# Two-layer encoder trunk on one core: a first phase with seven accumulators, six raw buffers and a fixed order

## The chip, the cores and the metric

The kernel runs on one core of a Trainium2 chip. The metric is the device time of one execution in microseconds (us). A core has five engines with instruction queues of their own: PE (matmul), DVE (elementwise, PSUM reads), ACT (activation functions, copies), POOL (elementwise on SBUF) and SP, which here only issues DMAs. An engine works through its queue strictly in the order in which the program was built, and waits at an instruction until its semaphores are up. Everything queued behind it waits too.

## The reference, cut to what matters

`x` is (1, 512, 1024). Layer 0 is built of a pooling mixer and a spatial-gating MLP, layer 1 of gated linear attention and stick-breaking attention. The change concerns the start of layer 0:

```python
def ada_modulate(x, c, norm_g, ada_w, ada_b):
    ada = jax.nn.silu(c) @ ada_w + ada_b
    shift, scale, gate = jnp.split(ada, 3, axis=-1)
    h = rmsnorm(x, norm_g) * (1.0 + scale[:, None, :]) + shift[:, None, :]
    return h, gate[:, None, :]

def even_layer(x, c, ...):
    h, gate_res = ada_modulate(x, c, norm_g, ada_w, ada_b)
    a, u, v, gate = _split(h @ in_w, EVEN_SIZES)
    ya = pool_mixer(a, pool_w, pool_scale)
    yb = spatial_gating(u, v, sgu_norm_g, sgu_w, sgu_b)     # u * (w . rmsnorm(v) + b)
    y = jnp.concatenate([ya, yb], axis=-1) * jax.nn.silu(gate)
    return x + gate_res * (y @ out_w)
```

So `h` (512 x 1024) is the left factor of one wide projection, and `ada` (a 1024-vector product per output column) must be there before `h` is. `u`, `v` and `gate` are column groups of that projection. `spatial_gating` normalises all of `v` (1024 columns) before it mixes tokens.

## The kernel before, in words

**Numbers.** The products are made in float32 accuracy out of reduced-precision matmuls: each operand is split into a high part (rounded, by ACT) and a low part (the difference, by DVE), and `mm3` issues three matmuls of 512 columns, high x high, high x low, low x high (lines L198, L199, L200). `split_w` (L184 on ACT, L185 on DVE) splits a weight tile into `whi` and `wlo`; `modulate` splits an activation tile into `hhi` (L305 or L307) and `hlo` (L308).

**First phase.** The contraction of 1024 is cut into eight k-tiles of 128. For each k-tile, `prepare(k)` does this: two `ada_block`s (each loads a 512 KB `raw` tile with the DMA of L167, and DVE reduces it against `sc`, the broadcast silu(c), with the custom operation of L174; L178 makes the scale `gcol`), one load of `wfirst` (768 columns: 512 of `v`, 256 of the gate) and its split, four transposes of the normalised x into an `aux` bank (L297), the modulation `h` (L301 or L303), `hhi` and `hlo`. Then 18 matmuls follow: four token blocks of `v` and two column blocks of the gate, each three matmuls, into six accumulators in the six `mm` banks of PSUM. `aux` has the two remaining banks. The `raw` tiles share four buffers, so a load is issued when the tile four loads earlier has been used up.

**Before the first phase** x comes in four token blocks (L149); ACT squares and sums each (L357), POOL turns the sum into 1/rms in two small operations (L282, L283), and DVE multiplies blocks 0 to 2 by it (L288), ACT block 3 (L362).

**After it** follow the other 512 columns of `v` (a unit of 96 matmuls in four accumulators), the 256 columns `u` of head group 0 (48 matmuls), then `gating` (eight float32 matmuls, L453, which read all four normalised blocks of `v`), `zs` on DVE and POOL (L456, L460) and the product with `u` (L464). Three more head groups and the pooling mixer go the same way, with further `ada_block`s put between the units as fillers, then the output projection and layer 1.

**What sets the order.** The program is written as straight code, and a scheduler orders the instructions of each engine when it is built, by its own estimate of times; it also decides which buffer a tile gets. On the chip nothing is reordered. Where the text says `manual_schedule`, the named engines keep the order in which the code is written.

Of the kernel before, what the change touches and what calls it, by code (L numbers as in the profile page):

```python
# [17 lines left out]
P = 128  # L18
# [21 lines left out]
def pack_inputs(i):  # L40
# [20 lines left out]
    g0 = 3072  # L61
    first = np.concatenate([w0[:, 2048:2560], w0[:, g0 + 1024:g0 + 1280]], axis=1).reshape(KT, P, 768)
# [35 lines left out]
def trunk(ctx: ExitStack, tc: tile.TileContext, d, out):  # L98
# [53 lines left out]
    for n in range(2):  # L152
        c = slice(n * 512, (n + 1) * 512)
        ps = bank("aux")
        T.matmul(ps, ones[0:1], c_row[0:1, c], start=True, stop=True)
        V.tensor_copy(out=sc[:, c], in_=ps)

# [132 lines left out]

    def modulate(l, k, tbs, xn):

        w = P * len(tbs)
        r = slice(tbs[0] * P, tbs[0] * P + w)
        ps = bank("aux")
        for i, t in enumerate(tbs):
            T.transpose(ps[:, i * P:(i + 1) * P], xn[t][:, k * P:(k + 1) * P], ident)  # L297
        h = slot("silu")
        g, b = gcol[:, 8 * l + k:8 * l + k + 1], ada[:, 24 * l + k:24 * l + k + 1]
        if l == 0 and k == 0:  # L300
            V.tensor_scalar(out=h, in0=ps, scalar1=g, scalar2=b, op0=ALU.mult, op1=ALU.add)  # L301
        else:
            A.activation(out=h[:, :w], in_=ps[:, :w], func=AF.Identity, scale=g, bias=b)  # L303
        if l or k:
            A.activation(out=h_hi[k][:, r], in_=h[:, :w], func=AF.Copy)  # L305
        else:
            V.tensor_copy(out=h_hi[k][:, r], in_=h[:, :w])  # L307
        V.tensor_tensor(out=h_lo[k][:, r], in0=h[:, :w], in1=h_hi[k].bitcast(F32)[:, r], op=ALU.subtract)  # L308

# [43 lines left out]

    xn = []
    for t in range(TB):
        n = big("n")
        A.activation(out=n, in_=x[t], func=AF.Square, accum_out=ss[:, t:t + 1])  # L357
        r = rms_scale(ss[:, t:t + 1], D)
        if t < TB - 1:
            normalise(t, r, n)  # L360
        else:
            A.mul(out=n, in_=x[t], mul=r)  # L362
        xn.append(n)

# [6 lines left out]
    v_ps = [bank() for _ in range(TB)]  # L371
    g_ps = [bank() for _ in range(2)]
    w_first = {}

    def prepare(k):
        ada_block(0, 8 + k)
        ada_block(0, k)
        w_first[k] = split_w(raw(d["wfirst"][k], 768), 768)
        modulate(0, k, range(TB), xn)
    prepare(0)  # L380
    for k in range(KT):
        if k + 1 < KT:
            prepare(k + 1)
        hi, lo = w_first.pop(k)
        for t in range(TB):
            r = slice(t * P, (t + 1) * P)
            mm3(v_ps[t], h_hi[k][:, r], h_lo[k][:, r], hi[:, :512], lo[:, :512], k == 0, k == KT - 1)
        for j in range(2):
            c = slice(512 + j * P, 512 + (j + 1) * P)
            mm3(g_ps[j], hi[:, c], lo[:, c], h_hi[k], h_lo[k], k == 0, k == KT - 1)  # L390

# [48 lines left out]
    for g in range(4):  # L440
# [380 lines left out]
```

## Time and profile before

| what | value |
|---|---|
| median of 3 runs | 865.55 us (864.79 to 869.39) |
| the profiled execution's own time | 867.59 us |
| its span, first to last instruction | 865.9 us |
| PE busy | 831.5 us, 96% |
| DVE, ACT, POOL busy | 503.0, 388.8, 82.1 us |
| DMA | 108.31 MB, 125 GB/s over the span |

PE is the engine to follow. Its busy time counts from issue to a modelled end, so that a matmul of 0.39 us that is followed by the next after 0.23 us counts as gapless work. The useful views are therefore the list of PE's waits, and the start times of its instructions, which show the pace. In a timeline a row gives the start, the duration, the engine, the line, the operation, what is written and read, and in brackets the idle time before it with what ended it. In the table by stretches a row gives the length, the busy time and the number of records of each engine, the granted clock of PE, and the share and rate of the DMA engines.

### The profile page before, as it was taken

How to read it: one execution, taken by the hardware profiler on the slowest of the kernel's cores; microseconds unless marked ns; L12 is line 12 of the kernel's file. 1: busy time of each engine (PE TensorE's matmuls, PEld its weight loads, DVE VectorE, ACT ScalarE, POOL GpSimd, SP SyncE). 2: the span in 40 equal slices, each digit the busy share in tenths (PEclk: the TensorE clock that was granted, in tenths of full speed). 3: DMA queues.
4: the chain of work that ended last, by engine and by line, in shares of the span. 5: the costliest groups of instructions: out<-in, count | busy, mean ns of one | idle time of the engine just before them, and what ended most of it. 6: DMA issues, size and time to landing. Idle time of an engine off the chain costs nothing.

```text
span 865.9 us, 10023 instructions
## 1 busy us (share of the span) xinstructions
PE 831.5 (96%) x3720; PEld 661.2 (76%) x3720; DVE 503.0 (58%) x801; ACT 388.8 (45%) x651; POOL 82.1 (9%) x139
## 2 busy tenths in 40 slices
PE   6999999999999999999999999989999998999996
PEld 3878888887888887787877778767676676888885
DVE  6856655588674478534628452473737567223775
ACT  5453212232343458534326252474737567433553
POOL 3002201100000000000000100020111111320011
PEclk9999999999999999999999999999999999999998
DMA  8885545554552355332201222212122111222362
GB/s 299 293 304 189 181 157 165 190 180 160 165 199 77 98 166 174 98 101 98 97 25 50 73 73 99 73 49 98 48 72 75 49 59 64 96 99 97 108 221 85
DMA packets 31363, 108.31 MB, mean 125 GB/s; under 512 B 3633, under 2 KB 3761, under 8 KB 31314
## 3 DMA queue, kind: packets, MB, share of 16 engines
q1 hardware_dynamic: 30738, 106.63, 37.1%
q10 hardware_dynamic: 576, 1.05, 0.3%
q8 instruction: 29, 0.48, 0.2%
q14 instruction: 20, 0.16, 0.1%
HBM read 105.56 MB, written 2.10 MB: 124 GB/s over the span
## 4 chain that ended last, share of the span: by engine, by line
PE 58%; DVE 14%; DMA 12%; ACT 6%; issue 5%; POOL 4%; SPq 0%; POOLq 0%; DVEq 0%; ACTq 0%
PE mm L199 16%; PE mm L200 16%; PE mm L198 16%; DMA raw<-in_adaT 9%; DVE wlo L185 4%; DVE sp L716 2%; PE aux L738 2%; DVE raw L174 2%; ACT whi L184 2%; DVE sp L711 2%; POOL sp L696 1%; DMA raw<-in_wfirst 1%; ACT sp L708 1%; PE aux L641 1%; PE aux L732 1%
## 5 line engine op out<-in xcount | busy, mean ns | idle before, releaser
L185 DVE TENSOR_TENSOR wlo<-raw,whi 128x1024 fp32r<-128x1024 f32 (+1 forms) x146 | 178.0, 1221 | 158.3 <-ACT whi L184 158.1
L184 ACT ACTIVATE whi<-raw 128x1024 fp32r<-128x1024 f32 (+1 forms) x146 | 152.5, 1044 | 205.9 <-PE mm L199 93.7
L200 PE MATMUL mm<-hhi,wlo 128*128 128x512 f32 x576 | 227.5, 395 | 1.9 <-DVE wlo L185 1.9
L198 PE MATMUL mm<-hhi,whi 128*128 128x512 f32 x576 | 227.5, 395 | 0.0
L199 PE MATMUL mm<-hlo,whi 128*128 128x512 f32 x576 | 227.1, 394 | 0.0
L200 PEld LDWEIGHTS mm<-hhi,wlo 128*128 128x128 f32 x576 | 108.8, 189 | 25.1 <-DVE wlo L185 2.3
L198 PEld LDWEIGHTS mm<-hhi,whi 128*128 128x128 f32 x576 | 108.9, 189 | 22.4 <-ACT misc L564 0.8
L199 PEld LDWEIGHTS mm<-hlo,whi 128*128 128x128 f32 x576 | 108.9, 189 | 22.3 <-issue 0.8
L174 DVE CUSTOM_DVE_ANT_0 raw<-raw,sc,cols 128x1024 f32<-128x1024 f32 x48 | 61.5, 1283 | 59.8 <-DMA raw<-in_adaT 59.7
L199 PE MATMUL mm<-wlo,hhi 128*128 128x512 f32 x192 | 76.5, 398 | 0.0
L198 PE MATMUL mm<-whi,hhi 128*128 128x512 f32 x192 | 76.3, 400 | 0.2 <-DVE hhi L307 0.2
L200 PE MATMUL mm<-whi,hlo 128*128 128x512 f32 x192 | 75.1, 399 | 0.5 <-DVE hlo L308 0.5
L200 PE MATMUL mm<-whi,r 128*128 128x512 f32 x160 | 62.6, 391 | 0.0
L198 PE MATMUL mm<-whi,r 128*128 128x512 f32 x160 | 62.5, 391 | 0.0
L199 PE MATMUL mm<-wlo,r 128*128 128x512 f32 x160 | 62.4, 390 | 0.0
L200 PEld LDWEIGHTS mm<-whi,hlo 128*128 128x128 f32 x192 | 36.7, 191 | 8.5 <-DVE hlo L308 1.3
L198 PEld LDWEIGHTS mm<-whi,hhi 128*128 128x128 f32 x192 | 36.6, 191 | 7.7 <-issue 0.6
L199 PEld LDWEIGHTS mm<-wlo,hhi 128*128 128x128 f32 x192 | 36.7, 191 | 7.5 <-DVE wlo L185 0.3
L190 DVE TENSOR_TENSOR r<-y,r 128x256 fp32r<-128x256 f32 (+1 forms) x60 | 29.5, 517 | 21.8 <-PE mm L199 16.2
L189 ACT ACTIVATE r<-y 128x256 fp32r<-128x256 f32 (+1 forms) x60 | 27.0, 479 | 29.0 <-PE mm L200 23.2
L282 POOL TENSOR_SCALAR rstd<-ssum 128x1 f32<-128x1 f32 x12 | 6.9, 574 | 307.8 <-DVE ssum L349 307.8
L199 PEld LDWEIGHTS mm<-wlo,r 128*128 128x128 f32 x160 | 30.1, 188 | 6.4 <-DVE wlo L185 0.3
(186 smaller groups left out, 1061.8 us busy)
## 6 DMA issues: line engine op xcount, KB each, us to landing
raw<-in_w SPq DMA_DIRECT2D x90, 512.0 KB, 3.3
raw<-in_adaT SPq DMA_DIRECT2D x48, 512.0 KB, 4.3
raw<-in_wo SPq DMA_DIRECT2D x48, 512.0 KB, 3.3
raw<-in_wfirst SPq DMA_DIRECT2D x8, 384.0 KB, 4.0
x<-in_x SPq DMA_DIRECT2D x4, 512.0 KB, 4.7
kq<-in_poolw SPq DMA_DIRECT2D x4, 256.0 KB, 4.5
out<-x SPq DMA_DIRECT2D x4, 256.0 KB, 2.6
out<-x ACTq DMA_DIRECT2D x4, 256.0 KB, 3.0
```

The costliest lines, as they stand in the source:

```text
L174: V.tensor_tensor_reduce(out=t, in0=t, in1=sc, scale=1.0, scalar=cols[:, C_AB[l] + b:C_AB[l] + b + 1], op0=ALU.mult, op1=ALU.add, accum_ou ...
L184: A.activation(out=hi[:, :w], in_=t[:, :w], func=AF.Copy)
L185: V.tensor_tensor(out=lo[:, :w], in0=t[:, :w], in1=hi.bitcast(F32)[:, :w], op=ALU.subtract)
L189: A.activation(out=hi, in_=src, func=AF.Copy)
L190: V.tensor_tensor(out=lo, in0=src, in1=hi.bitcast(F32), op=ALU.subtract)
L198: T.matmul(o, lh, rh, start=start, stop=False)
L199: T.matmul(o, lh, rl, start=False, stop=False)
L200: T.matmul(o, ll, rh, start=False, stop=stop)
L641: T.matmul(ov, gv[p][:, 512 * c + c0:512 * c + c0 + P], att[:, j * P:(j + 1) * P], start=True, stop=p == 0)
L711: V.scalar_tensor_tensor(out=sp[:, :w], in0=z[:, :w], scalar=0.0, in1=sp[:, :w], op0=ALU.max, op1=ALU.add)
L716: V.tensor_tensor_scan(out=r, data0=ones[:, 0:1].to_broadcast([P, n]), data1=r, initial=0.0, op0=ALU.mult, op1=ALU.add)
L738: T.matmul(ps[:, s * P:], sv[s][:, hd * P:(hd + 1) * P], wt[s], start=s == 0, stop=s == 3)
```

## The change

The diff cut to its core (the packing of the weights on the host follows from it: `wfirst` gets 128 columns of `u`, and the tile of `u` for head group 0 keeps the other 128):

```diff
-        V.tensor_copy(out=sc[:, c], in_=ps)
+        if n:
+            A.copy(out=sc[:, c], in_=ps)
+        else:
+            V.tensor_copy(out=sc[:, c], in_=ps)
...
-    def modulate(l, k, tbs, xn):
+    def modulate(l, k, tbs, xn, between=lambda t: None):
...
         for i, t in enumerate(tbs):
+            between(t)
             T.transpose(ps[:, i * P:(i + 1) * P], xn[t][:, k * P:(k + 1) * P], ident)
-        h = slot("silu")
+        h = slot("misc" if l == 0 else "silu")
...
             V.tensor_copy(out=h_hi[k][:, r], in_=h[:, :w])
-        V.tensor_tensor(out=h_lo[k][:, r], in0=h[:, :w], in1=h_hi[k].bitcast(F32)[:, r], op=ALU.subtract)
+            between(TB)
+        E = V if l else G
+        E.tensor_tensor(out=h_lo[k][:, r], in0=h[:, :w], in1=h_hi[k].bitcast(F32)[:, r], op=ALU.subtract)
...
+        if t % 2:
+            V.tensor_tensor_reduce(out=xn[t], in0=x[t], in1=x[t], scale=1.0, scalar=0.0, op0=ALU.mult, op1=ALU.add,
+                                   accum_out=ss[:, t:t + 1])
+        else:
+            A.activation(out=xn[t], in_=x[t], func=AF.Square, accum_out=ss[:, t:t + 1])
...
-    g_ps = [bank() for _ in range(2)]
+    g_ps = [bank(), bank(), bank("aux")]
+    def idle_work(n):
+        for _ in range(n):
+            T.matmul(v_ps[0][:, :P], ident, ident, start=True, stop=True)
 
     def prepare(k):
...
+        if k == 0:
+            t = raw(d["wfirst"][k], 896)
+            def between(i):
+                if i == TB:
+                    w_first[k] = split_w(t, 896)
+                elif i == TB - 1:
+                    idle_work(6)
+            modulate(0, k, range(TB), xn, between)
+            idle_work(10)
...
+    with tc.manual_schedule(engines={T.engine}):
+        with tc.manual_schedule(engines={V.engine, A.engine}):
+            prepare(0)
+            prepare(1)
+        for k in range(KT):
+            if 0 < k < KT - 1:
+                prepare(k + 1)
+            if k:
+                for o in first_products(k):
+                    mm3(*o, False, k == KT - 1)
+                continue
+            ops = first_products(k)
...
+    u_first = slot("y")
+    V.tensor_copy(out=u_first, in_=g_ps[2])
...
+            hi, lo = nxt()
+            ps = bank()
+            for k in range(KT):
+                c = slice(k * P, (k + 1) * P)
+                mm3(ps, hi[:, c], lo[:, c], h_hi[k], h_lo[k], k == 0, k == KT - 1)
+            gating()
+            V.tensor_tensor(out=u_first, in0=u_first, in1=zs[0], op=ALU.mult)
+            y[8] = u_first
+            u_evac(1, ps)
...
-BUFS = {"big": 5, "y": 16, "kq": 8, "z": 4, "sp": 3, "r": 7, "misc": 3, "silu": 2, "raw": 4, "w": 3}
+BUFS = {"big": 5, "y": 16, "kq": 8, "z": 4, "sp": 3, "r": 7, "misc": 3, "silu": 2, "raw": 6, "w": 3}
...
-    nc = _bacc.Bacc("TRN2", target_bir_lowering=False, num_devices=1)
+    nc = _bacc.Bacc("TRN2", target_bir_lowering=False, num_devices=1, dynamic_dma_scratch_size=2048)
```

In words. (1) A seventh accumulator, in one of the two `aux` banks, takes 128 columns of `u` along in the first phase: 24 matmuls move there from the unit of head group 0, which is left with 24. (2) `raw` has six buffers instead of four; the memory comes from a smaller DMA scratch area. (3) In layer 0 `hlo` is made on POOL. (4) Squares of x blocks 1 and 3, with their sums, are made on DVE, and the second half of `sc` is copied by ACT. (5) PE's order is fixed through the first phase, and DVE's and ACT's for k-tiles 0 and 1. For k-tile 0 all seven accumulators first get high x high, then the products that read `wlo`, and those that read `hlo` last. (6) 16 float32 matmuls of the identity with itself, whose results are overwritten, stand on PE: six ahead of the last transpose of k-tile 0, ten behind it.

The first place is the beginning of PE's queue. Here `aux<-ident,n` is a transpose of one x block (`n`) and `mm_158<-ident` the identity product; whi and hhi are the high parts. Before:

```order
L297 MATMUL aux_177<-ident,n_146 128x128
L297 MATMUL aux_199<-ident,n_146 128x128
L297 MATMUL aux_177<-ident,n_152 128x128
L297 MATMUL aux_199<-ident,n_152 128x128
L297 MATMUL aux_239<-ident,n_134 128x128
L297 MATMUL aux_239<-ident,n_140 128x128
L297 MATMUL aux_239<-ident,n_146 128x128
L297 MATMUL aux_239<-ident,n_152 128x128
L198 MATMUL mm_158<-whi_173,hhi_118 128x512
L199 MATMUL mm_158<-wlo_174,hhi_118 128x512
```

And now:

```order
L304 MATMUL aux_178<-ident,n_136 128x128
L389 MATMUL mm_158<-ident 128x128 x6
L304 MATMUL aux_178<-ident,n_137 128x128
L389 MATMUL mm_158<-ident 128x128 x10
L304 MATMUL aux_220<-ident,n_134 128x128
L304 MATMUL aux_220<-ident,n_135 128x128
L304 MATMUL aux_220<-ident,n_136 128x128
L304 MATMUL aux_220<-ident,n_137 128x128
L432 MATMUL mm_158<-whi_192,hhi_118 128x512
L432 MATMUL mm_159<-whi_192,hhi_118 128x512
```

The transposes of k-tile 1 no longer alternate with those of k-tile 0; they stand behind the ten identity products, ahead of the first product, and those of k-tile 2 have moved behind the products of k-tile 0.

The second place is the beginning of DVE's queue, up to the modulation of k-tile 0 (`n` is a normalised x block, the ISA rows on `raw` are the ada reductions, those on `n,ss` the new squares). Before:

```order
L156 COPY sc_94<-aux_108 128x512
L288 TENSOR_SCALAR n_134<-x_98,rstd_136 128x1024
L156 COPY sc_94<-aux_111 128x512
L288 TENSOR_SCALAR n_140<-x_99,rstd_142 128x1024
L288 TENSOR_SCALAR n_146<-x_100,rstd_148 128x1024
L174 ISA raw_164,ada<-raw_164,sc_94,cols 128x1024
L174 ISA ada 128x1
L174 ISA raw_168,ada<-raw_168,sc_94,cols 128x1024
```

And now:

```order
L162 COPY sc_94<-aux_108 128x512
L366 ISA n_135,ss<-x_99 128x1024
L366 ISA ss 128x1
L294 TENSOR_SCALAR n_134<-x_98,rstd_139 128x1024
L294 TENSOR_SCALAR n_135<-x_99,rstd_144 128x1024
L294 TENSOR_SCALAR n_136<-x_100,rstd_149 128x1024
L366 ISA n_137,ss<-x_101 128x1024
L366 ISA ss 128x1
L180 ISA raw_169,ada<-raw_169,sc_94,cols 128x1024
L180 ISA ada 128x1
L184 SCALAR_TENSOR_TENSOR gcol<-ada,cols 128x1
L180 ISA raw_173,ada<-raw_173,sc_94,cols 128x1024
```

The square of block 3 stands behind the three normalisations, and the first ada reduction behind that square.

The third place is DVE's queue at the end of the second half of `v` (`ssum` adds the two halves of a token's sum of squares, `v<-v,rstd` normalises a block). Before, behind the copy of block 3:

```order
L401 COPY v_488<-mm_514 128x512
L437 TENSOR_SCALAR v_486<-v_486,rstd_651 128x1024
L349 TENSOR_TENSOR ssum_655<-ss 128x1
L174 ISA raw_824,ada<-raw_824,sc_94,cols 128x1024
L174 ISA ada 128x1
L437 TENSOR_SCALAR v_487<-v_487,rstd_657 128x1024
L349 TENSOR_TENSOR ssum_661<-ss 128x1
L185 TENSOR_TENSOR wlo_760<-raw_757,whi_759 128x1024
L437 TENSOR_SCALAR v_488<-v_488,rstd_663 128x1024
```

And now:

```order
L451 COPY v_535<-mm_563 128x512
L358 TENSOR_TENSOR ssum_704<-ss 128x1
L191 TENSOR_TENSOR wlo_807<-raw_804,whi_806 128x1024
L489 TENSOR_SCALAR v_534<-v_534,rstd_706 128x1024
L358 TENSOR_TENSOR ssum_710<-ss 128x1
L180 ISA raw_998,ada<-raw_998,sc_94,cols 128x1024
L180 ISA ada 128x1
L489 TENSOR_SCALAR v_535<-v_535,rstd_712 128x1024
```

On PE the eight gating matmuls stood 48 matmuls behind the end of the unit of `v`; they now stand 24 behind it. From the gating on, PE's queue is the same, row for row, to the end of the program, and so are all but a few rows of ACT's and DVE's (fillers and splits that change places). SP's queue has the same loads; some fillers and pooling weights change places with weight tiles.

More of the change, by code (lines that the diff above doesn't have):

```diff
@@ L61, in pack_inputs @@
     g0 = 3072
[L62 removed]
+    first = np.concatenate([w0[:, 2048:2560], w0[:, g0 + 1024:g0 + 1280], w0[:, 1024:1152]],
+                           axis=1).reshape(KT, P, 896)
     s0 = [t_tiles(w0, 2560)]
@@ L351, in token_rstd @@
         return rms_scale(s, D)
-    xn = []
+    xn = [big("n") for _ in range(TB)]
     for t in range(TB):
-        n = big("n")
-        A.activation(out=n, in_=x[t], func=AF.Square, accum_out=ss[:, t:t + 1])
+        if t % 2:
+            V.tensor_tensor_reduce(out=xn[t], in0=x[t], in1=x[t], scale=1.0, scalar=0.0, op0=ALU.mult, op1=ALU.add,
+                                   accum_out=ss[:, t:t + 1])
+        else:
+            A.activation(out=xn[t], in_=x[t], func=AF.Square, accum_out=ss[:, t:t + 1])
         r = rms_scale(ss[:, t:t + 1], D)
         if t < TB - 1:
-            normalise(t, r, n)
+            normalise(t, r, xn[t])
         else:
-            A.mul(out=n, in_=x[t], mul=r)
-        xn.append(n)
+            A.mul(out=xn[t], in_=x[t], mul=r)
     def silu_to(dst):
@@ L377, in prepare, with first_products @@
         ada_block(0, k)
[L378 to L383, printed above, removed]
+        if k == 0:
[7 more added lines that the diff above has]
+            idle_work(10)
+        else:
+            w_first[k] = split_w(raw(d["wfirst"][k], 896), 896)
+            modulate(0, k, range(TB), xn)
+    def first_products(k):
         hi, lo = w_first.pop(k)
+        ops = []
         for t in range(TB):
             r = slice(t * P, (t + 1) * P)
-            mm3(v_ps[t], h_hi[k][:, r], h_lo[k][:, r], hi[:, :512], lo[:, :512], k == 0, k == KT - 1)
-        for j in range(2):
+            ops.append((v_ps[t], h_hi[k][:, r], h_lo[k][:, r], hi[:, :512], lo[:, :512]))
+        for j in range(3):
             c = slice(512 + j * P, 512 + (j + 1) * P)
-            mm3(g_ps[j], hi[:, c], lo[:, c], h_hi[k], h_lo[k], k == 0, k == KT - 1)
+            ops.append((g_ps[j], hi[:, c], lo[:, c], h_hi[k], h_lo[k]))
+        return ops
+    with tc.manual_schedule(engines={T.engine}):
[10 more added lines that the diff above has]
+            ops = first_products(k)
+            for ps, lh, ll, rh, rl in ops:
+                T.matmul(ps, lh, rh, start=True, stop=False)
+            for ps, lh, ll, rh, rl in ops[:TB]:
+                T.matmul(ps, lh, rl, start=False, stop=False)
+            for ps, lh, ll, rh, rl in ops[TB:]:
+                T.matmul(ps, ll, rh, start=False, stop=False)
+            for ps, lh, ll, rh, rl in ops[:TB]:
+                T.matmul(ps, ll, rh, start=False, stop=False)
+            for ps, lh, ll, rh, rl in ops[TB:]:
+                T.matmul(ps, lh, rl, start=False, stop=False)
     V.tensor_copy(out=ones_r, in_=ones)
@@ L467, in trunk @@
             gating()
-        c_unit(nxt, u_evac, gating if g == 0 else lambda: None)
+        if g:
+            c_unit(nxt, u_evac)
+        else:
+            hi, lo = nxt()
[7 more added lines that the diff above has]
+            u_evac(1, ps)
         fillers(2)
```

3 lines of the change are left out of this document (2 added, 1 removed).

## The prediction

> **What bounds the kernel now.** I read the page first, then the list of PE's waits, then PE's start times in the first 60 us, then the table by stretches, and at last DVE, POOL and ACT around the two places where PE waits.
>
> ```profile
> PE 831.5 (96%) x3720; PEld 661.2 (76%) x3720; DVE 503.0 (58%) x801; ACT 388.8 (45%) x651; POOL 82.1 (9%) x139
> ...
> PE aux L732 <- POOL z L696: 7.1, 4, 2.6
> ...
> PE aux L297 <- DVE n L288: 2.4, 5, 0.8
> PE mm L200 <- DVE wlo L185: 1.9, 1, 1.9
> ...
> PE mm L200 <- DVE hlo L308: 0.5, 2, 0.3
> ```
>
> PE works for 96% of the span. Its longest wait, at L732, belongs to the stick-breaking attention, which the change doesn't touch; L297 are transposes, most of them at the start. Two others lie near the change: 0.5 us for hlo, 1.9 us once for wlo. DMA does not appear, so the first phase is not bound by loads, though they fill 90% of the DMA engines there (below). Moving matmuls into that phase can therefore fill no gap: the gain must come from the start or from those two waits.
>
> ```profile
> 13.24 0.69 PE L297 MATMUL aux<-ident,n 128*128 128x128 f32 x2 [2.09 <-ACT n L362]
> ...
> 15.91 0.77 PE L198 MATMUL mm<-whi,hhi 128*128 128x512 f32 x1 [0.18 <-DVE hhi L307]
> ...
> 18.61 0.63 PE L198 MATMUL mm<-whi,hhi 128*128 128x512 f32 x1
> 19.03 0.63 PE L199 MATMUL mm<-wlo,hhi 128*128 128x512 f32 x1
> ...
> 21.00 0.39 PE L198 MATMUL mm<-hhi,whi 128*128 128x512 f32 x1
> 21.23 0.40 PE L199 MATMUL mm<-hlo,whi 128*128 128x512 f32 x1
> ...
> 54.36 1.07 PE L198 MATMUL mm<-whi,hhi 128*128 128x512 f32 x4
> ```
>
> The first product starts at 15.91. Until about 20.7 products start 0.42 us apart, from then on 0.23 us. The one at 21.00 is the thirteenth (by the order, behind twelve products of v). At full pace twelve take 12 x 0.227 = 2.7 us, so this stage ends as if it had begun at 21.0 - 2.7 = 18.3 at full pace. The first phase is over at 54.36, when the next unit starts without a gap.
>
> ```profile
> 17.29:20.70 3.41, 3.41 (x9) 1.00 0.84 273
> 205.02:208.43 3.41, 1.52 (x8) 1.00 0.00 0
> 208.43:211.85 3.42, 3.42 (x8) 0.51 0.41 153
> 211.85:215.26 3.41, 3.41 (x16) 0.99 0.86 262
> ...
> 20.70:54.36 33.66, 33.20 (x154) 1.00 0.90 310
> ```
>
> In these rows (PE's busy time, its records, its granted clock, DMA) the clock changes in steps of 3.41 us. After a stretch with 1.52 us of work in 3.41, PE gets half the clock for one stretch and does 8 matmuls where 15 or 16 fit: 7 x 0.23 = 1.6 us lost on top of the wait. (The clock's record begins at 20.7; the 1.00 in the first row is none, as its 9 records show.)
>
> **The change, part by part.** *The moved matmuls* (24 x 0.227 = 5.4 us) cost and gain nothing: PE has no gap where they leave nor where they go. The first phase alone would end at 54.36 + 5.4 = 59.8 with them. The loads grow to 1.51 MB a k-tile (two of 512 KB, one of 448), at 310 GB/s 4.9 us, under the 21 x 0.227 + 0.4 = 5.2 us of PE: hidden.
>
> *The start.* The last x block decides when transposing ends.
>
> ```profile
> 9.07 0.55 POOL L283 TENSOR_TENSOR rstd<-rstd,mhalf 128x1 f32<-128x1 f32 x1
> ...
> 9.80 0.65 POOL L282 TENSOR_SCALAR rstd<-ss 128x1 f32<-128x1 f32 x1 [0.18 <-ACT n L357]
> 10.32 1.28 DVE L174 CUSTOM_DVE_ANT_0 raw<-raw,sc,cols 128x1024 f32<-128x1024 f32 x1
> ...
> 10.54 1.47 POOL L283 TENSOR_TENSOR rstd<-rstd,mhalf 128x1 f32<-128x1 f32 x1
> ...
> 12.04 1.15 ACT L362 ACTIVATE n<-x,rstd 128x1024 f32<-128x1024 f32 x1 [2.33 <-POOL rstd L283]
> ```
>
> POOL's L283 takes 0.55 us, but 1.47 under DVE's L174: it gets in when that ends. Now block 3 is squared on DVE behind the third normalisation. That one ends at 10.3 in the trace, where L174 begins, and some 0.5 later now, since the square of block 1 stands ahead of all three; with the 1.28 of a row like L174 the square ends near 12.1. ACT ended it at 9.7 before (POOL starts at 9.80). POOL's two operations follow under the ada reductions. If L282 waits one out (12.1 + 1.2) and L283 gets in at once, 1/rms is there at 13.9; if both wait, at 15.1; if neither, at 13.0. ACT adds 1.2: the last transpose at 14.2 to 16.4, and I take 15.7 (it is nearest to the row with 1.47). Behind it: the transpose 0.3 (from 13.24 on a pair takes 0.69), ten identity products, four transposes 0.4 (estimated from 0.23 for 512 columns, twice for their short form).
>
> ```profile
> 87.21 1.95 PE L453 MATMUL aux<-kq,v 128*128 128x128 f32 x16
> 88.91 0.48 PE L198 MATMUL mm<-hhi,whi 128*128 128x512 f32 x1
> ```
>
> Sixteen records are eight float32 matmuls, and 1.70 / 8 = 0.21 us each at full clock. Ten are 2.1, six at half clock some 2.4. The first product starts at 15.7 + 0.3 + 2.1 + 0.4 = 18.5 at full pace, against 18.3: **-0.2 us**. Bounds: +1.3 (transpose at 14.2) and -3.0 (at 16.4, and ten identity products at half clock, +2.1). Its h and hhi hide under the identity products, 0.8 + 0.4 behind the transpose:
>
> ```profile
> L301 DVE TENSOR_SCALAR silu<-aux,gcol,ada 128x512 f32<-128x512 f32 x1 | 0.8, 811 | 0.9 <-PE aux L297 0.9
> L307 DVE CAST hhi<-silu 128x512 fp32r<-128x512 f32 x1 | 0.4, 421 | 0.0
> ...
> 18.94 0.78 ACT L303 ACTIVATE silu<-aux,ada,gcol 128x512 f32<-128x512 f32 x1 [1.26 <-DVE ada L174]
> 19.75 0.63 ACT L305 ACTIVATE hhi<-silu 128x512 fp32r<-128x512 f32 x1
> ```
>
> *The waits for hlo* of the list fall away, since PE's order no longer puts those products early for a k-tile that is late: **+0.5**. *The small edits*, the second half of sc on ACT, one copy of u more on DVE and h in another pool, cost nothing: ACT stands idle ahead of 12.04 and DVE works 58% of the span. The copy of sc would cost if it came after 12.1, when the first reduction needs it; ACT can start it near 8.5, behind its second square.
>
> *hlo on POOL.*
>
> ```profile
> 93.86 2.55 POOL L460 TENSOR_TENSOR z<-z,silu 128x512 f32<-128x512 f32 x2 [8.74 <-DVE z L456]
> ...
> 106.54 1.94 DVE L185 TENSOR_TENSOR wlo<-raw,whi 128x1024 fp32r<-128x1024 f32 x1
> ...
> L174 DVE CUSTOM_DVE_ANT_0 raw<-raw,sc,cols 128x1024 f32<-128x1024 f32 x16 | 20.4, 1281 | 3.1 <-DMA raw<-in_adaT 3.1
> L185 DVE TENSOR_TENSOR wlo<-raw,whi 128x768 fp32r<-128x768 f32 x8 | 8.0, 995 | 1.6 <-ACT whi L184 1.5
> ```
>
> The same shape on POOL takes 1.3 us, and the row at 106.54 shows that it isn't taken from DVE for nothing: this split ran beside a POOL operation and took 1.94 instead of 1.22 (207.15 below). The two engines take turns. So per k-tile DVE and POOL together need 2 x 1.28 + 1.16 (896 columns) + 1.3 = 5.0 us, with gcol and the hand-overs some 5.2, where PE needs 5.2: level, 0. Only k-tile 1 is late. From the last transpose at 16.0: h and hhi 17.2, wlo 18.4, hlo of k-tile 0 19.7, two reductions and gcol 22.4, h and hhi of k-tile 1 on ACT (0.8 + 0.6) 23.8, hlo on POOL 25.1, or 26.3 if it waits out a reduction. PE asks for it at 18.5 + 4.8 + 0.4 + 0.5 = 24.2: a wait of 0.9 to 2.1, 0 if DVE is quicker than its durations. I take **-1.0**.
>
> *The gating.*
>
> ```profile
> 76.10 0.39 PE L200 MATMUL mm<-whi,hlo 128*128 128x512 f32 x1
> ...
> 83.39 1.10 POOL L282 TENSOR_SCALAR rstd<-ssum 128x1 f32<-128x1 f32 x1 [0.95 <-DVE ssum L349]
> ...
> 85.15 0.76 DVE L437 TENSOR_SCALAR v<-v,rstd 128x1024 f32<-128x1024 f32 x1 [0.72 <-POOL rstd L283]
> ```
>
> Block 3 of v is normalised 9.8 us after the last product of v, and gating reads it at 87.21, 11.1 after. With 24 matmuls fewer between, PE gets there 5.7 + 0.6 us after. In the new order (third place above) I count from that product: DVE, in order, normalises blocks 0 and 1 first, so the copy of block 3 ends near 2.5, ssum and a split 3.7 (POOL waits it out), L283 4.3, normalisation of block 2 5.0, ssum, a reduction that POOL again waits out 6.3, L283 7.0, normalisation of block 3 7.8. The wait is 7.8 - 6.3 = 1.5, none if POOL gets in first, 3 if a filler's load is late. I take **-1.2**. Behind the waiting matmul stands the whole of PE's queue.
>
> *Six raw buffers.*
>
> ```profile
> 192.40 1.63 SPq L167 DMA_DIRECT2D raw<-in_adaT  x2
> ...
> 196.87 1.29 DVE L174 CUSTOM_DVE_ANT_0 raw<-raw,sc,cols 128x1024 f32<-128x1024 f32 x1 [3.20 <-DMA raw<-in_adaT]
> ...
> 207.15 1.22 DVE L185 TENSOR_TENSOR wlo<-raw,whi 128x1024 fp32r<-128x1024 f32 x1
> 208.43 0.73 PE L200 MATMUL mm<-hhi,wlo 128*128 128x512 f32 x1 [1.89 <-DVE wlo L185]
> ```
>
> PE's 1.9 us end with a split that came late because DVE, in order, had stood 3.2 us before a filler's load; and that load was issued only at 192.40, when a buffer came free. With six buffers it waits for a tile used two loads earlier and is there before DVE. DVE gains more than 1.9, so the wait goes, **+1.9** (0 is the other bound), and with it the stretch at half clock, 1.6. Whether a wait of 1.9 in 3.41 drops the clock depends on where it falls among the stretches. I count half, **+0.8**: the profiled execution took 867.59 us (865.89 of span and 1.7 around), the median run 2.0 less, about one such stretch.
>
> [...]
>
> **Sum**: -0.2 + 0.5 - 1.0 - 1.2 + 1.9 + 0.8 = 0.8 us gained, 865.55 - 0.8 = **864.8**. (From the profiled execution, with its clock stretch counted in full: 867.59 - 1.6 = 866.0.)
>
> **Rivals.** *Faster, the start and the covers hold*: POOL gets in at once, the last transpose is at 14.2, hlo and the gating find their operands. +1.3 + 0.5 + 0 + 0 + 1.9 + 1.6 = 5.3, 860.3 us. For it: every wait I count is of 1 to 2 us and hangs on which of two engines comes first. Against: all must go well together.
>
> *Slower, POOL starves beside DVE*: in the first phase hlo loses its turn to two DVE operations in a row, as one L282 here did:
>
> ```profile
> 840.22 1.70 POOL L282 TENSOR_SCALAR rstd<-ssum 128x1 f32<-128x1 f32 x1 [3.55 <-DVE ssum L349]
> ```
>
> Then the chain per k-tile is 5.2 + 1.3 against PE's 5.2. It decides once POOL loses more than about 0.6 us in each of seven k-tiles; at 0.9 they cost 6.3 in place of 1.0, and the sum is -4.5: 870.1 us. Against: the 1.47 row got in between two reductions.
>
> [...]
>
> *The clock doesn't rise in time*: six identity products are 2.4 us of work, and two to three idle microseconds follow before the last transpose. If that leaves the clock low, the start is at its bound, -3.0; the wait for hlo is then covered: -3.0 + 0.5 - 1.2 + 1.9 + 0.8 = -1.0, 866.6 us. [...]
>
> **How the numbers follow.** Forecast 0.47, faster rival 0.28, clock rival 0.15, slower rival 0.10. About 0.5% (4.3 us) is what a measurement of this kernel can tell from no change. Forecast and clock rival lie within it: same 0.62, faster 0.28, slower 0.10. The range 859.8 to 869.2 leaves out the outer part of each rival, about 0.1 on either side.
>
> **What would show it.** The first phase: products 0.23 apart from the first on, starting near 18.5, and the next unit near 60 (59 to 62). A wait of L206 for POOL's hlo at k-tile 1 and of L505 for L489 of about a microsecond each. No wait of PE near 208 (there about 0.5 to 1 later), no stretch at half clock there, and DVE's waits for adaT far below now. The forecast is wrong if PE waits for hlo at every k-tile, if the first products are 0.42 apart, or if the wait for wlo stays.

## The result: slower by 0.46%

The changed kernel takes 870.1 us (median of 20 runs, 866.55 to 873.7), the kernel before 866.07 (20 runs beside them, 863.77 to 870.02). The ratio is 1.0046, with a 95% interval of 1.0031 to 1.0062: 2.7 to 5.4 us slower. The forecast was 864.8 us, too near to be told from no change.

The profiled execution after was the shortest of the 20: 866.55 us, span 864.8, with no stretch at half clock but the one at the end that every trace has. That of the kernel before (867.59, span 865.9) had two more, near 208 and near 635, at some 1.6 us each. Read end against end, the changed kernel would look a microsecond faster. So the two traces have to be compared place by place.

The list of PE's waits of the changed kernel (us in total, times, longest):

```profile
PE aux L795 <- POOL z L759: 7.3, 4, 2.6
...
PE aux L505 <- DVE v L489: 2.6, 2, 2.2
...
PE mm L205 <- DVE wlo L191: 0.2, 1, 0.2
```

The attention (L795, L732 before) is as it was. The waits for hlo and the 1.9 us for wlo are gone. New is L505, the gating, which waits for v.

PE's timeline at the start (start, duration, what, number of records; an identity matmul has two here):

```profile
11.35 2.77 PE L389 MATMUL mm<-ident 128*128 128x128 f32 x12
15.29 0.47 PE L304 MATMUL aux<-ident,n 128*128 128x128 f32 x1 [1.17 <-ACT n L374]
15.55 4.07 PE L389 MATMUL mm<-ident 128*128 128x128 f32 x20
19.45 0.60 PE L304 MATMUL aux<-ident,n 128*128 128x128 f32 x4
...
60.92 0.39 PE L204 MATMUL mm<-whi,hhi 128*128 128x512 f32 x1
```

The last transpose is at 15.3 (forecast 15.7), but the ten identity matmuls take 3.9 us, 0.39 each where the gating has 0.21 at full clock: half clock. The next unit starts at 60.92; in the trace of the kernel before it starts at 54.36, and 54.36 + 5.4 = 59.8.

The gating, with DVE, POOL and PE in order of time:

```profile
77.13 1.28 DVE L180 CUSTOM_DVE_ANT_0 raw<-raw,sc,cols 128x1024 f32<-128x1024 f32 x1 [2.81 <-DMA raw<-in_adaT]
79.15 1.28 DVE L180 CUSTOM_DVE_ANT_0 raw<-raw,sc,cols 128x1024 f32<-128x1024 f32 x1 [0.73 <-DMA raw<-in_adaT]
...
82.34 0.19 POOL L288 TENSOR_SCALAR rstd<-ssum 128x1 f32<-128x1 f32 x1 [27.90 <-DVE ssum L358]
82.46 0.39 PE L206 MATMUL mm<-whi,hlo 128*128 128x512 f32 x1
...
85.64 0.69 DVE L451 COPY v<-mm 128x512 f32<-128x512 f32 x1
...
86.31 1.22 DVE L191 TENSOR_TENSOR wlo<-raw,whi 128x1024 fp32r<-128x1024 f32 x1
86.48 1.10 POOL L288 TENSOR_SCALAR rstd<-ssum 128x1 f32<-128x1 f32 x1 [1.54 <-DVE ssum L358]
...
88.13 0.60 PE L505 MATMUL aux<-kq,v 128*128 128x128 f32 x4
...
88.98 1.28 DVE L180 CUSTOM_DVE_ANT_0 raw<-raw,sc,cols 128x1024 f32<-128x1024 f32 x1
89.15 1.16 POOL L288 TENSOR_SCALAR rstd<-ssum 128x1 f32<-128x1 f32 x1 [0.94 <-DVE ssum L358]
90.97 0.75 DVE L489 TENSOR_SCALAR v<-v,rstd 128x1024 f32<-128x1024 f32 x1 [0.71 <-POOL rstd L289]
91.78 1.38 PE L505 MATMUL aux<-kq,v 128*128 128x128 f32 x10 [2.25 <-DVE v L489]
92.92 0.47 PE L204 MATMUL mm<-hhi,whi 128*128 128x512 f32 x1
```

The last product of the unit of v starts at 82.46. The copy of block 3 of v ends 3.9 us after it (86.33), where I had counted 2.5: DVE had stood 2.81 and 0.73 us before fillers' loads. POOL's L288 takes 0.2 us alone (82.34) and then twice 1.1, until the DVE operation that began just before it is over.

The gating takes 4.79 us from its first matmul (88.13) to the next product (92.92); in the kernel before, where it has no wait, 88.91 - 87.21 = 1.70. So it costs 3.1 us, of which the list of waits shows 2.6. Behind it the changed kernel is 4.0 us late (92.92 against 88.91), 0.9 of them brought along. Near 218 it is only 0.2 late: near 208 the kernel before loses 3.8 us, with its wait of 1.9 and the half-clock stretch behind it.

### The profile page after: what moved, and what is told of

Same layout as the page of the kernel before. It is cut to its first block, busy times and chain, and to the rows that moved or that the text cites. A ratio compares the mean times of both kernels' runs of the same rounds, so it can differ in the third digit from the quotient of the medians.

```text
span 864.8 us, 10089 instructions
## 1 busy us (share of the span) xinstructions
PE 830.2 (96%) x3752; PEld 663.9 (77%) x3752; DVE 507.6 (59%) x796; ACT 387.3 (45%) x647; POOL 97.2 (11%) x147
## 3 DMA queue, kind: packets, MB, share of 16 engines
q10 hardware_dynamic: 576, 1.05, 0.3%
## 4 chain that ended last, share of the span: by engine, by line
PE 77%; DVE 9%; ACT 6%; POOL 3%; issue 3%; DMA 2%; SPq 0%; POOLq 0%; ACTq 0%; DVEq 0%
PE mm L205 22%; PE mm L206 21%; PE mm L204 21%; DVE sp L779 2%; DVE wlo L191 2%; PE aux L801 2%; ACT whi L190 2%; DVE sp L774 2%; POOL sp L759 1%; ACT sp L771 1%; PE aux L704 1%; PE aux L795 1%; PE aux L304 1%; POOL rstd L288 1%; PE aux L505 1%
## 5 line engine op out<-in xcount | busy, mean ns | idle before, releaser
L204 PE MATMUL mm<-hhi,whi 128*128 128x512 f32 x566 | 222.6, 393 | 0.0
L206 PE MATMUL mm<-hhi,wlo 128*128 128x512 f32 x566 | 222.2, 393 | 0.0
L205 PE MATMUL mm<-hlo,whi 128*128 128x512 f32 x566 | 222.2, 393 | 0.0
L205 PEld LDWEIGHTS mm<-hlo,whi 128*128 128x128 f32 x566 | 106.5, 188 | 21.8 <-issue 0.8
L206 PEld LDWEIGHTS mm<-hhi,wlo 128*128 128x128 f32 x566 | 106.3, 188 | 22.0 <-issue 0.8
L204 PEld LDWEIGHTS mm<-hhi,whi 128*128 128x128 f32 x566 | 106.4, 188 | 21.8 <-ACT misc L627 0.8
L180 DVE CUSTOM_DVE_ANT_0 raw<-raw,sc,cols 128x1024 f32<-128x1024 f32 x48 | 68.2, 1430 | 49.1 <-DMA raw<-in_adaT 49.1
L204 PE MATMUL mm<-whi,hhi 128*128 128x512 f32 x188 | 74.2, 394 | 0.0
L205 PE MATMUL mm<-wlo,hhi 128*128 128x512 f32 x188 | 73.8, 393 | 0.0
L288 POOL TENSOR_SCALAR rstd<-ssum 128x1 f32<-128x1 f32 x12 | 6.9, 574 | 308.4 <-DVE ssum L358 308.4
```

Of the source, the lines that this page charges most:

```text
L180: V.tensor_tensor_reduce(out=t, in0=t, in1=sc, scale=1.0, scalar=cols[:, C_AB[l] + b:C_AB[l] + b + 1], op0=ALU.mult, op1=ALU.add, accum_ou ...
L204: T.matmul(o, lh, rh, start=start, stop=False)
L205: T.matmul(o, lh, rl, start=False, stop=False)
L206: T.matmul(o, ll, rh, start=False, stop=stop)
L288: G.tensor_scalar(out=r, in0=ssq, scalar1=1.0 / n, scalar2=EPS, op0=ALU.mult, op1=ALU.add)
```

## The experiments

"Ratio" is always to the kernel before, run beside them on the same chip, with a 95% interval. The median of the kernel before there was 866 to 867 us. Line numbers move by a few between versions; the names tell.

### Is it the gating? Moved by 48 matmuls, then by 24

```diff
-            gating()
-            V.tensor_tensor(out=u_first, in0=u_first, in1=zs[0], op=ALU.mult)   # and the rest of u
+            owed.append(later)                        # the same lines, run in the next unit:
...
-            c_unit(nxt, silu_to(sg))
+            c_unit(nxt, silu_to(sg), owed.pop())      # e1: behind its 48 matmuls; silu 4, raw 5 buffers
+            c_unit(nxt, silu_to(sg), half=owed.pop()) # e5: between its halves; buffers unchanged
```

> The changed kernel, except that the gating of head group 0 comes 96 matmuls later (behind the gate columns of group 1), with four silu buffers and five raw buffers to make room. Theory (the loss is the wait in the gating, 2.6 us, and a stretch at half clock that this wait triggers in some executions, 1.6 us each): no wait above 0.3 us ahead of the gating; 870.1 - 2.6 = 867.5, less up to 1.6 for the stretch, so 866.0 to 867.5. Rival (the loss is at the start or in the first phase, the wait is given back later): 869.5 to 870.5.

(The unit has 48 matmuls; the 96 are a slip.) Measured: 870.76 us, ratio 1.0044 (1.0021 to 1.0067), as slow as the changed kernel. That would have spoken for the rival, but the trace of this version (PE, then DVE) shows another wait of the same size:

```profile
105.19 3.08 PE L506 MATMUL aux<-kq,v 128*128 128x128 f32 x14 [2.57 <-DVE z L509]
...
103.18 1.28 DVE L180 CUSTOM_DVE_ANT_0 raw<-raw,sc,cols 128x1024 f32<-128x1024 f32 x1 [4.83 <-DMA raw<-in_adaT]
104.39 1.41 DVE L509 SCALAR_TENSOR_TENSOR z<-aux,cols,kq 128x512 f32<-128x512 f32 x2
```

Two gatings now follow each other with two aux banks between them, and DVE, which must empty the first, stands 4.8 us before a filler's load. So this run decides nothing about the old wait.

> The changed kernel, except that the gating of head group 0 stands 24 matmuls (5.4 us) later, between the two halves of the next unit, so that the two gatings do not follow each other; buffers as in the changed kernel. Theory (of the 3.5 to 4 us that the changed kernel is slower, 2.6 are the wait in the gating and about 0.8 the half-clock stretches that it triggers): v is normalised at 91.7 and the gating now starts near 93.5, no wait; 3 us less than the changed kernel, so within 1 us of the kernel before. Rival (the time is lost elsewhere and any wait here only shows it): no change, 3 to 4 us slower than the kernel before.

Measured: 865.16 us, ratio 0.9996 (0.9981 to 1.0011). In its trace v is ready at 92.8 and the gating runs without a wait:

```profile
92.03 0.75 DVE L491 TENSOR_SCALAR v<-v,rstd 128x1024 f32<-128x1024 f32 x1 [0.70 <-POOL rstd L291]
...
94.01 1.95 PE L508 MATMUL aux<-kq,v 128*128 128x128 f32 x16
```

Here too the gating takes 1.70 us to the next product. One edit, which leaves the start, the first phase, POOL's hlo and the buffers as they are, takes the whole loss away. The loss comes in at the gating: shown.

### Undoing the seventh accumulator

```diff
-    first = [... w0[:, 1024:1152]] 896 columns; g_ps = [bank(), bank(), bank("aux")]
+    first = [...] 768 columns;                  g_ps = [bank(), bank()]
-        E = V if l else G                       # hlo
+        E = V
         (u of head group 0 a whole unit again, its gating behind it)
```

> The changed kernel without its seventh accumulator: wfirst is 768 columns wide again, u of head group 0 is a whole unit, and hlo is made on DVE; the start, the fixed order, the identity matmuls and the six raw buffers stay. Theory: 72 instead of 48 matmuls stand before the gating again, so it doesn't wait; against the kernel before, the start costs 1.5 us, the waits for hlo (0.5) and near 208 (1.9) are gone: 866.1 + 1.5 - 2.4 = 865.2, less about 0.8 for the half-clock stretch of the kernel before near 208: 864.4 (863.5 to 866). Rival (the start and the fixed order carry the loss): 868 to 870.

(The 72 and 48 are a slip too: 48 and 24.) Measured: 866.4 us, ratio 1.0006 (0.9987 to 1.0025): not slower, and the gating has no wait:

```profile
87.54 1.95 PE L500 MATMUL aux<-kq,v 128*128 128x128 f32 x16
```

The start, the fixed order and the identity matmuls don't carry the loss. The gain over the kernel before that I expected (864.4 us) isn't there either; which of its terms was wrong is not shown.

### What makes v late

```diff
+        last_v = V.tensor_scalar(out=v[t], ...)
     def fillers(n):
+        with tc.issue_after(last_v.ins):
```

> The changed kernel with the fillers (the later ada reductions) held back until v is normalised; nothing else. Theory (DVE reaches the copies of v late because it stands 3.5 us before fillers' loads, and a filler splits the last chain on POOL): the wait in the gating shrinks from 2.6 to 0 to 1.0 us, and the time by 1.6 to 3 us. Rival (the chain through POOL alone takes too long): the wait stays above 1.8 us.

Measured: 869.85 us, ratio 1.0032 (1.0014 to 1.0051). The wait in the gating is gone altogether, and yet the time hardly moves. PE, and DVE before it, in this version:

```profile
88.14 1.95 PE L507 MATMUL aux<-kq,v 128*128 128x128 f32 x16
...
199.09 1.28 DVE L180 CUSTOM_DVE_ANT_0 raw<-raw,sc,cols 128x1024 f32<-128x1024 f32 x1 [2.75 <-DMA raw<-in_adaT]
...
209.18 1.22 DVE L191 TENSOR_TENSOR wlo<-raw,whi 128x1024 fp32r<-128x1024 f32 x1
210.45 0.50 PE L206 MATMUL mm<-hhi,wlo 128*128 128x512 f32 x1 [2.12 <-DVE wlo L191]
```

The cause of the wait is shown: the fillers put ahead of v. Their work on DVE is owed, though. DVE now stands 2.75 us before a filler's load at 199.09 and works without a gap from there to the split at 209.18, which is late near the place where the kernel before had waited too. The wait is given back.

### The start, piece by piece

Three edits of the changed kernel, one each:

```diff
e3   -  idle_work(6) ... idle_work(10)
     +  idle_work(0) ... idle_work(0)
e9   -  6 ahead of the last transpose, 10 behind
     +  2, 2, 2, 10 ahead of the four transposes, 3 behind
e6   -  if t % 2: V.tensor_tensor_reduce(...) else: A.activation(Square)
     +  A.activation(Square) for every t
```

> The changed kernel without the sixteen matmuls on the identity, all else the same. Theory (they cost more than they give, since the ten run at half clock, 3.9 us, and hold the first product until 19.8): the first product starts near 17.2, the products 0.42 us apart until the clock rises, some 3.4 us later; the first phase ends 0.5 to 1.5 us earlier, 868.6 to 869.6. Rival (they raise the clock earlier than products would): the first phase ends later by 0.5 to 1.5 us, 870.6 to 871.6.

Measured: 870.44 us, ratio 1.0043 (1.0022 to 1.0064). The first product started at 17.3 and ran at half clock until 21.0 (from 19.1 on 0.43 us apart); the gain of either side is too small to see. Whether the sixteen identity matmuls help or harm cannot be told. Its trace shows what the wait in the gating can bring on top. By stretches of the clock (length, PE busy and records, ..., granted clock):

```profile
89.28:92.69 3.41, 1.21 (x11) 1.21 (x11) 2.70 (x6) 0.00 (x0) 1.27 (x2) 1.00 0.61 217
92.69:96.10 3.41, 3.41 (x10) 2.66 (x9) 2.60 (x3) 0.00 (x0) 2.51 (x2) 0.50 0.45 157
```

> The changed kernel with its identity matmuls put elsewhere: 2, 2, 2 and 10 ahead of the four transposes of the first k-tile and 3 behind them, in place of 6 ahead of the last and 10 behind; nothing else. Theory (the ten ran at half clock because PE had rested about a microsecond ahead of each transpose, so that no stretch before them was worked through; work without gaps ahead of the transposes lifts the clock by 13): the first product starts near 17 at full pace, 2.8 us earlier, and the kernel is 2 to 3 us faster than the changed kernel, 0.5 to 1.5 us slower than the kernel before; the wait in the gating stays at 2.6. Rival (an earlier first phase only makes the first products wait for POOL's hlo and for the loads): under 1 us faster than the changed kernel.

Measured: 871.17 us, ratio 1.0057 (1.0039 to 1.0075). The clock was up by 11.4 (from there ten identity matmuls take 2.41 us, where the ten of the changed kernel take 4.07) and the first product started at 17.1 at full pace, as expected. The gain went at once:

```profile
24.97 0.75 PE L206 MATMUL mm<-whi,hlo 128*128 128x512 f32 x1 [1.05 <-POOL hlo L317]
...
21.64:25.06 3.42, 1.98 (x10) 0.89 (x8) 3.42 (x4) 2.25 (x3) 1.71 (x1) 1.00 0.86 290
25.06:28.47 3.41, 3.41 (x8) 2.70 (x9) 3.41 (x7) 1.41 (x2) 0.78 (x1) 0.50 0.93 325
```

PE waits 0.4 us for the transposes' bank and 1.05 for POOL's hlo, and a stretch at half clock costs some 1.6: 3.0 us in all, more than the 19.8 - 17.1 = 2.7 gained. Here the rival I named was right. The wait in the gating was not 2.6, as expected, but 3.2, with a stretch at half clock behind it.

> The changed kernel with all four blocks of x squared on ACT, as before. Theory (the square of block 3 on DVE makes the last transpose late, 15.3 against 13.2): the last transpose starts near 13.5, the first product near 17.5 to 18, the first phase ends 1.5 to 2 us earlier, and the whole is 1.5 to 2 us faster than the changed kernel (2 us slower than the kernel before). Rival (the rise of the clock sets the start, not the transpose): the identity matmuls then run at half clock throughout, the first product starts near 18 and the gain is under 0.8 us.

Measured: 873.04 us, ratio 1.0079 (1.0058 to 1.01), slower still, but not a clean test. Without the squares the scheduler put a reduction ahead of the third normalisation on DVE, where it waits for its load:

```profile
11.06 1.28 DVE L180 CUSTOM_DVE_ANT_0 raw<-raw,sc,cols 128x1024 f32<-128x1024 f32 x1 [2.20 <-DMA raw<-in_adaT]
...
12.27 0.75 DVE L294 TENSOR_SCALAR n<-x,rstd 128x1024 f32<-128x1024 f32 x1
```

So the last transpose was no earlier (15.90), and the wait in the gating grew to 3.2 us.

### hlo on DVE

```diff
-        E = V if l else G
+        E = V
```

> The changed kernel with hlo of layer 0 on DVE again, nothing else. Theory (hlo on POOL is neither a cost nor a gain: the trace shows no wait of PE for it, DVE's longer reductions are hidden): within 1 us of the changed kernel, 3 to 4.5 us slower than the kernel before, the wait in the gating 2 to 3 us. Rival (POOL and DVE in turns make DVE late for the whole first phase, and so for the fillers and for v): the wait in the gating shrinks by a microsecond or more, and the time with it.

Measured: 868.94 us, ratio 1.0022 (1.0005 to 1.0039). That is 1.9 us slower than the kernel before, less than the 3 to 4.5 expected, but the interval overlaps that of the changed kernel. The gating waits 2.8 us, so the rival (POOL makes DVE late for v) falls; whether a microsecond is gained cannot be told.

### More traces of the two kernels

> The changed kernel once more, for another profiled execution. Theory: in most executions a stretch of 3.4 us at half clock follows the wait in the gating (near 93), at a cost of 1.6 us, and the ten identity matmuls take 3.9 to 4.5 us, at half clock for the most part. Rival: no stretch there; the lower mean clock comes from stretches in the attention (560 to 740), which both kernels have.

> The same kernel as in look a, and the same expectation: in at least two of the three looks a stretch at half clock near 93. Rival: in none.

> The same kernel as in looks a and b, and the same expectation.

Measured, in the traces a, b and c: spans of 864.9, 867.5 and 867.0. The gating waits 2.2 to 2.6 us in each (4.55, 4.84 and 4.58 us to the next product), and none of the three has a stretch at half clock behind it; that expectation fell. Traces b and c have two such stretches in the attention, near 684 and 732, as the rival said. The start is of two kinds. In trace a, as in the first trace, the ten identity matmuls ran at half clock (4.0 us). In b and c they ran at full clock (2.40 us). PE in trace c:

```profile
15.54 2.40 PE L389 MATMUL mm<-ident 128*128 128x128 f32 x20
17.78 0.60 PE L304 MATMUL aux<-ident,n 128*128 128x128 f32 x4
18.13 1.17 PE L432 MATMUL mm<-whi,hhi 128*128 128x512 f32 x4
...
25.04 0.50 PE L206 MATMUL mm<-whi,hlo 128*128 128x512 f32 x1 [0.95 <-POOL hlo L317]
```

The first product comes at 18.1, and then PE waits 0.95 us for POOL's hlo of k-tile 1. In the first trace and in trace a, where it comes at 19.81 and 20.11, PE has no such wait. The next unit starts at 60.43 and 60.66 where the identity matmuls ran at full clock, at 60.92 and 61.20 where they ran at half clock.

The kernel before, unchanged, twice:

> The kernel before once more, for another profiled execution. Theory (the wait for wlo near 208 hangs on when a load lands, and is not in every execution): the wait near 208 is under 1 us or absent in at least one of two looks. Rival (it is in every execution, 1.5 to 2.3 us): then the missing 1 to 2 us stay unexplained. The clock should rise near 19.3 to 22.7 in both, since products run without a gap from 15.9.

> The same kernel as in the first of the two looks, and the same expectation.

Measured: spans of 862.3 and 870.0. The wait for wlo near 208 is in both, and longer than in the first trace (here the wait, and the first row of the next unit, of the one and then of the other):

```profile
PE mm L200 <- DVE wlo L185: 2.1, 1, 2.1
...
53.73 1.07 PE L198 MATMUL mm<-whi,hhi 128*128 128x512 f32 x4
...
PE mm L200 <- DVE wlo L185: 2.7, 1, 2.7
...
56.02 1.20 PE L198 MATMUL mm<-whi,hhi 128*128 128x512 f32 x4
```

So that term is a real gain, and the theory that it comes and goes falls. The clock rose at 19.7 and 20.8, as expected. But the first phase of the unchanged kernel ends at 53.73, 54.36 or 56.02, so that one trace is no firm base for the price of a start.

The first of these two has no stretch at half clock but the one at its end, like the first trace of the changed kernel. These two can be set end against end: 864.8 - 862.25 = 2.6 us. By place: the first phase ends at 60.92 against 53.73 + 5.44 = 59.17 (+1.75), the gating takes 4.79 against 1.70 (+3.1), and near 208 the kernel before loses 2.2. That sums to 2.6.

### Six raw buffers alone, and what is best

```diff
e4    kernel before with "raw": 6 and dynamic_dma_scratch_size=2048
e8    e4, and idle_work(4), (1), (2), (6) ahead of the four transposes of k-tile 0, (3) behind
e10   e5 and e9 together
e12   e10 with the squares on ACT, the first reductions held behind the third normalisation,
      4, 1, 2, 6 ahead
e13   e12 with hlo on DVE
```

> The kernel before with six raw buffers in place of four and the smaller DMA scratch, nothing else. Theory: the filler's load comes in time, PE's wait of 1.9 us near 208 is gone, and with it the stretch at half clock in those executions that had it: 866.1 - 1.9 = 864.2, less 0 to 1.6: 863.4 (862.5 to 864.3). Rival (the wait only moves on, to the next late tile): 865.5 to 866.5.

Measured: 864.82 us, ratio 0.9979 (0.9956 to 1.0002). No wait of PE for wlo above 0.3 us; the time agrees with the 1.9 us, though the interval reaches no change.

> The kernel before with six raw buffers, and identity matmuls ahead of the transposes of the first k-tile (4, 1, 2 and 6 ahead of the four blocks) and three behind them, so that PE works without a gap from about 6.3 to 14; six accumulators, hlo and squares as before. Theory (the clock rises after about 3.4 us of unbroken work, so here before the first product at 16): products 0.23 us apart from the first on, 2 to 2.4 us less than with six raw buffers alone, which was 2.2 us below the kernel before: 4 to 4.6 us below the kernel before, about 862.5. Rival (the identity matmuls don't lift the clock, as the ten of the changed kernel didn't): first products 0.42 apart, same as six raw buffers alone, 864.8.

Measured: 861.92 us, ratio 0.9949 (0.9923 to 0.9975), the lowest median of all. PE by stretches, and its first products:

```profile
7.59:11.00 3.41, 3.41 (x18) 3.41 (x18) 2.57 (x4) 1.97 (x4) 2.65 (x5) 1.00 1.02 404
...
15.78 0.47 PE L198 MATMUL mm<-whi,hhi 128*128 128x512 f32 x1 [0.63 <-DVE hhi L308]
16.08 0.40 PE L199 MATMUL mm<-wlo,hhi 128*128 128x512 f32 x1
16.31 0.39 PE L198 MATMUL mm<-whi,hhi 128*128 128x512 f32 x1
```

PE worked without a gap in one stretch, the clock's record begins at its end (11.0), and the products run 0.23 us apart from the second on. PE waits 1.2 us for wlo at 203, where the version with six raw buffers and no identity matmuls had no such wait.

> Both repairs of the changed kernel together: the gating of head group 0 between the halves of the next unit, and the identity matmuls 2, 2, 2, 10 ahead of the transposes and 3 behind. Theory: 3.5 us (gating and its half-clock stretches) and 2.8 us (start) add up: about 6 us faster than the changed kernel, some 2.5 us below the kernel before, 863.5 to 864.5. Rival (the earlier start brings a wait elsewhere, as the wait for wlo near 203 to 208 came back in the warm-start version of the kernel before): 865 or more.

Measured: 867.53 us, ratio 1.0018 (1.0002 to 1.0033). The two repairs don't add up: the first product is at 17.0, but PE waits 1.05 us for POOL's hlo again, as the rival said.

> The version with the gating in mid unit and the warm start, with the squares of x all on ACT as in the kernel before, the first reductions on DVE held behind the third normalisation, and 4, 1, 2, 6 identity matmuls ahead of the transposes and 3 behind. Theory (DVE's square of block 3 costs the start 2 us): the last transpose near 13.3, the first product near 15.5 at full pace, 1.5 us earlier than with DVE's squares; about 862.5, at or below the best so far (861.9). Rival (the loads of the first k-tiles then bind): first products wait for wlo or hlo of k-tile 1, no gain.

Measured: 863.75 us, ratio 0.9972 (0.9953 to 0.9991). The first product starts at 15.3, the wait for hlo is still 1.05.

> The version with the gating in mid unit, the warm start and the squares on ACT, with hlo on DVE in place of POOL. Theory (POOL's hlo of k-tile 1 is what took the warm start's gain back): PE's wait of 1.05 us for hlo near 23 goes, 1 to 2.5 us less than with hlo on POOL: 861.3 to 862.8. Rival (DVE is late for hlo of k-tile 1 too, behind reductions whose loads are late): the wait stays, 863.5 or more.

Measured: 862.65 us, ratio 0.9967 (0.9949 to 0.9986). PE's wait for hlo falls to 0.55. With seven accumulators this is the best, and no better than six with a warm start (e8).

## Why the prediction was wrong

Its terms (gain positive), beside what the traces show:

| step | predicted | measured |
|---|---|---|
| start | -0.2 (+1.3 to -3.0) | with the next two: -0.7 between the means of four traces and three; +1.0 to -2.0 by pairs |
| waits for hlo before | +0.5 | 0.5, 0 and 0.3 in the three traces before; gone |
| hlo on POOL, k-tile 1 | -1.0 | -1.0 in two traces, 0 in two (hidden by a later start) |
| gating | -1.2 (0 to -3) | -2.9 to -3.1 in the four traces, 2.2 to 2.6 of it in the list of waits |
| wait near 208 | +1.9 | +1.9 to +2.7 |
| half clock near 208 | +0.8 | in two of three traces before; behind the waiting gating in four of eight traces |

**The step that failed is the gating: its price, and its clock.** My count gave a wait of 1.5 us with POOL behind a DVE operation twice, and I took 1.2 in case POOL got in first. POOL got in first neither time (1.10 and 1.16). And a filler's load was late (2.81 and 0.73), so that the copy of block 3 ended 3.9 us after the last product of v, and not the 2.5 that the count starts from. The row at 196.87 of the profile before, DVE 3.2 us before such a load, had shown that this happens. Nor did six raw buffers end it: I expected DVE's waits for adaT to be far below, and over the span they went from 59.7 us in 30 waits to 49.1 in 22, the longest 4.7 in both. The gating cost 2.9 to 3.1 us; the bound of -3 was the better value.

And I counted the half-clock stretch on one side only. I gave the removed wait of 1.9 us half a stretch, +0.8, and the added wait, of the same kind, none. In eight traces in which the gating waits for v (four of the changed kernel, four of versions of it), four have the stretch behind it, all four of versions; in the three traces of the kernel before, two have it near 208. So I put this term at about 0, an estimate from few traces. With -3.0 and 0 in their places the sum is -0.2 + 0.5 - 1.0 - 3.0 + 1.9 + 0 = -1.8, 867.4 us, in place of 864.8. The signs by which I wanted to know the forecast wrong (hlo at every k-tile, first products 0.42 apart, the wait for wlo) all stayed away: none of them looked at the gating.

**What held.** The start: "I take 15.7" came at 15.3, "first product starts at 18.5" at 18.13 and 18.35 in the two traces with the clock up by then, at 19.81 and 20.11 in the two without, within the bounds given. The start with the two terms for hlo was forecast at -0.7 and came out so in the mean, though the traces scatter so much that this is partly luck. The wait for POOL's hlo at k-tile 1, "a wait of 0.9 to 2.1", was 0.95 and 0.97 where the start was early, and covered where it was late, as the clock rival said. The moved matmuls cost nothing in the first phase: PE has no gap there between 26 and 61. The wait near 208 went. DVE and POOL took turns (POOL's L288 took 0.19 us alone, 1.10 and 1.16 beside a DVE operation), but PE waits for POOL's hlo at k-tile 1 at most, so POOL doesn't starve: that the rival's time, 870.1, is the measured one is luck, for the mechanism was another.

**What stays open.** The rows explain 1.4 us by the means of the traces (-0.7 - 3.0 + 2.25) and 2.6 in the one pair without a stretch at half clock; the comparison says 4.0 (2.7 to 5.4). Another 0.5 of the miss in the time lies in the base, 866.07 us in place of 865.55. Part of the difference lies in the clock: over the runs the mean granted clock was 0.9927 after and between 0.9937 and 0.9945 before (beside the experiments, on four chips), and one stretch more lowers it by 1.7 / 865 = 0.002 (1.7 is half of 3.41). Against the middle, 0.9941, that is 0.7 stretches, 1.1 us. Within the 20 runs of the changed kernel, a line through spans and clocks gives 1.6 us per 0.002.

Which stretches these are is not shown. The version with the gating in mid unit points to those behind the gating: its mean clock was 0.9947, one stretch above the changed kernel's, and its ratio fell by 1.0046 - 0.9996 = 0.5%, 4.3 us, where the wait alone is worth 3.0. Against it, the four traces of the changed kernel itself have none there (two of them have theirs in the attention), and taking the wait near 208 from the kernel before left its mean clock as it was (0.9937 with six raw buffers, 0.9937 beside it).

## What to carry to other kernels

A wait that is moved must be counted with everything that hangs on it, on both sides: if a removed wait is credited with a stretch at half clock, an added one of its size is charged with one. Work taken from between a producer and its reader (here 24 matmuls between v and the gating) is cover; the chain behind it is priced with its late loads in, since DVE, which takes fillers in order, stood 2.75 to 4.83 us before one of them in the traces above. And a faster start is worth only what the next producer (here POOL's hlo, DVE's split at 203) can follow: five versions lost a part or all of it there, in waits of 0.55 to 1.2 us.

## What the runs showed of the hardware

In the traces the granted clock changed in stretches of 3.413 us, which kept their grid (the times at which one ends and the next begins) through an execution: in the kernel before, the half-clock stretches near 208 and 635 are 3.413 us each, and the 423.25 us between them are 124 such stretches. From trace to trace the grid lay differently: the clock's record begins at 20.79 there, at 19.04 in the first trace of the changed kernel. Stretches at half clock stood behind stretches in which PE had worked little, 1.52 us ahead of the one near 208, 1.21 in e3 ahead of the one at 92.69. In the 20 traces (one for each run, and those of the two kernels) 38 stretches at half clock were counted, those at the end of each trace left out; in the stretch ahead of it PE was busy for 0.5 to 1.7 us of 3.41 in 37 cases, for 1.98 in one (e9 at 21.64, above). Of the others, those between 20 and 800 us, only three with less than 1.7 kept the clock (1.51 to 1.65). So whether a wait of 2.2 us cost a stretch hung on where the grid fell: in e3 one of 2.25 us lay in the stretch from 89.28 and did. In the changed kernel the same wait was cut in two:

```profile
87.32:90.73 3.41, 1.90 (x11) 1.36 (x9) 2.23 (x5) 1.06 (x1) 2.30 (x4) 1.00 0.48 154
90.73:94.14 3.41, 2.35 (x15) 2.16 (x16) 3.17 (x5) 0.00 (x0) 0.60 (x2) 1.00 0.58 171
94.14:97.56 3.42, 3.42 (x16) 2.82 (x15) 2.60 (x3) 0.63 (x1) 2.15 (x2) 1.00 0.38 137
```

1.90 and 2.35 us of work, and no stretch at half clock. Over the runs, the line through spans and clocks gives 1.6 us per 0.002 for the changed kernel (above), and 1.0 to 1.8 for the versions with twelve runs. An estimate of the chance: if the grid lies anywhere with equal chance, a single wait of w us, longer than 1.7, holds half a stretch with a chance of w / 3.41, which is 0.66 for 2.25 us and 0.55 for 1.89. Four of eight and two of three were counted, too few to prove it.

What made the clock rise stays open. In trace b it rose behind a stretch with 2.75 us of work, the identity matmuls among it; with six raw buffers alone it did not rise behind one with 3.02, of transposes and first products, but only behind the next.
